# Second feed-forward weights by seven products per 2x2 block, and PSUM as one pool of banks

## The chip, the core and the metric

The kernel runs on one core of a Trainium2 chip. The core has a matrix engine (TensorE, PE in the profile, with its weight loads apart as PEld), VectorE (DVE), ScalarE (ACT), GpSimd (POOL) and SyncE (SP), which here only issues DMAs. Matrix products accumulate in PSUM, eight banks of 128 partitions by 512 fp32 numbers; everything else lives in SBUF. The metric is the device time of one execution in microseconds, the median of the runs.

## The reference, cut to what matters

Two blocks of two layers each work on x of 512 tokens by 1024 columns. Every layer has a mixer (convolution or attention) and then a feed-forward part; the first block also attends to a memory. The change is in the second products of the feed-forward parts (`@ w2`, `@ w_down`); their inner dimension is 4096 (`D_FF`) in the first block and 2816 (`D_FF_2`) in the second.

```python
def sqrelu_mlp(h, w1, w2):
    return jnp.square(jax.nn.relu(h @ w1)) @ w2

def swiglu(h, w_gate, w_up, w_down):
    return (jax.nn.silu(h @ w_gate) * (h @ w_up)) @ w_down

def first_block(...):
    for l in range(DEPTH):
        x = x + (conformer_conv(...) if l < N_A_LAYERS else fox_attention(...))
        x = x + memory_cross_attention(rmsnorm(x, norm_mem_g[l]), ...)
        x = x + sqrelu_mlp(rmsnorm(x, norm_ff_g[l]), ff_w1[l], ff_w2[l])
    return rmsnorm(x, final_norm_g)

def second_block(x, ...):
    for i in range(DEPTH):
        h = rms_norm(x, mix_norm[i])
        x = x + (short_conv_mixer(h, ...) if i % 2 == 0 else dilated_attention_mixer(h, ...))
        x = x + swiglu(rms_norm(x, ffn_norm[i]), ffn_w_gate[i], ffn_w_up[i], ffn_w_down[i])
    return rms_norm(x, final_norm)
```

## The kernel before

x stays in SBUF, transposed, as eight tiles `x0` to `x7` of 128 columns of the model by 512 tokens. Every fp32 operand of a large product is split in two numbers that the matrix engine takes at full rate, hi (the rounded value, a cast on ScalarE) and lo (the rest, a subtraction on VectorE): weights in `split_weights` (L163; `whi`, `wlo`, cast L169, subtraction L170), activations in `split_act` and `split_into` (L222 to L224; `ahi`, `alo`). `mm3` (L173) then makes one product of three matmuls, hi by hi, hi by lo, lo by hi, so that 24 matmuls of 512 columns make a block of 128 output columns from 1024 inputs.

`gemm_steps` goes over pairs of such output blocks. For a pair it loads 1 MB of weights from HBM (`load_weights`, tile `raw`, three buffers, issued by SP), splits it into four hi/lo tiles (two slots with two buffers each) and runs the products. `ff_sqrelu` works through the hidden dimension in four chunks of 1024: for each, the first weights give eight hidden tiles (evacuation L706, Square on ScalarE L708, split L224), and the second weights add the chunk's share to x (evacuation `residual`, L593: x = PSUM + x). `swiglu` does the same with gate and up weights, in chunks of 8, 8 and 6 hidden tiles. The norm's factor is computed while the first products run: at step 13 of the first gemm of a layer PE sums squares, POOL raises to the power -1/2 (`rtm`, L278), and at step 18 PE spreads the result over the partitions; every evacuation needs it.

PE runs its matmuls in the order in which the program writes them. The other engines' orders are made by a scheduler ahead of time from its own estimates; within an engine instructions start in that order, and a waiting instruction holds up all behind it. PSUM is opened anew by `banks(g, s, t)` where a stage starts: then the first matmul of the stage waits until the last bank of the stage before has been read.

The fox attention (`heads_attention`) starts with the splits of x without gain; the gains of its norm are multiplied into the weights instead (`gained`, L782, POOL; `fr`, L1119, POOL, for the forget gate's weights, which L1123 on VectorE finishes as tile `fw`).

## Time and profile before

| what | value |
|---|---|
| median of the three runs | 2654.21 us (2652.49 to 2655.27) |
| the profiled execution, its time | 2655.16 us |
| its span in the trace | 2653.4 us |
| granted TensorE clock, mean | 0.997 |
| PE busy | 2600.3 us, 98% |
| PEld busy | 2178.7 us, 82% |
| DVE busy | 1489.7 us, 56% |
| ACT busy | 1097.9 us, 41% |
| POOL busy | 548.8 us, 21% |

The span is the part of the execution that the trace covers; 1.76 us lie around it. Matmuls are pipelined, and each row of a matmul is drawn longer than the distance to the next one, so the distance between starts is what a matmul costs.

### The profile page before, as it was taken

To read this page: it belongs to the slowest core of one execution; us is meant where nothing else is said; L and a number is where in the kernel's file an instruction comes from. 1 tells how busy PE (TensorE), PEld (TensorE's weight loads), DVE (VectorE), ACT (ScalarE), POOL (GpSimd) and SP (SyncE) were. 2 spreads that over 40 slices of the span, in tenths; PEclk is the share of its full clock that TensorE was granted. 3 is DMA by queue.
4 is the path that set the end of the run, shared out by engine and by line. 5 is a ranking of instruction groups with operands and counts; after the bars stand their busy time and mean duration, and the time that the engine had idled before them with its cause. 6 is when DMAs were issued, how large, how long until landed. Compare 5 with 4: busy or idle time off the path is not lost.

```text
span 2653.4 us, 32283 instructions
## 1 busy us (share of the span) xinstructions
PE 2600.3 (98%) x12521; PEld 2178.7 (82%) x12521; DVE 1489.7 (56%) x2215; ACT 1097.9 (41%) x1843; POOL 548.8 (21%) x585
## 2 busy tenths in 40 slices
PE   8999999999999999999999999999999999999999
PEld 6889888888878787888888788888888888788888
DVE  6995564433557887554344665433335777643333
ACT  6755443322437675342223322322224666422223
POOL 5862110000226532110000511211112221211111
PEclk9999999999999999999999999999999999999999
DMA  7255133333322222233333393333324232233331
GB/s 211 78 194 181 56 96 96 98 103 101 95 74 72 80 96 72 72 111 96 95 97 96 87 166 109 90 100 101 96 83 119 85 88 88 77 96 98 96 87 56
DMA packets 319320, 264.82 MB, mean 100 GB/s; under 512 B 6980, under 2 KB 304512, under 8 KB 319168
## 3 DMA queue, kind: packets, MB, share of 16 engines
q1 hardware_dynamic: 316112, 258.15, 33.4%
q10 hardware_dynamic: 2480, 4.33, 0.5%
q8 instruction: 99, 1.62, 0.3%
q0 software_dynamic: 576, 0.28, 0.1%
q14 instruction: 53, 0.43, 0.1%
HBM read 251.16 MB, written 11.57 MB: 99 GB/s over the span
## 4 chain that ended last, share of the span: by engine, by line
PE 82%; DVE 6%; POOL 4%; issue 4%; ACT 2%; DMA 1%; SPq 0%; ACTq 0%; POOLq 0%; DVEq 0%
PE ps_g L92 76%; PE ps_s L92 3%; POOL pa L433 2%; PE ps_t L92 2%; PE ps_t L95 1%; DVE wlo L170 1%; DVE ps_s L425 1%; DVE alo L236 1%; DVE x L593 1%; POOL sall L994 1%; POOL raw L782 0%; DVE x L938 0%; DMA raw<-in_conv_pw_w 0%; DVE wlo L795 0%; DVE x L1286 0%
## 5 line engine op out<-in xcount | busy, mean ns | idle before, releaser
L92 PE MATMUL ps_g<-ahi,whi 128*128 128x512 f32 x3052 | 1195.2, 392 | 10.8 <-DVE x L593 5.8
L92 PE MATMUL ps_g<-alo,whi 128*128 128x512 f32 x3052 | 1188.0, 389 | 1.6 <-DVE alo L236 1.6
L92 PE MATMUL ps_g<-ahi,wlo 128*128 128x512 f32 x3052 | 1188.0, 389 | 0.0
L169 ACT CAST whi<-raw 128x1024 fp32r<-128x1024 f32 (+2 forms) x384 | 384.1, 1007 | 1163.1 <-PE ps_g L92 1103.3
L92 PEld LDWEIGHTS ps_g<-ahi,whi 128*128 128x128 f32 x3052 | 574.7, 188 | 129.6 <-issue 11.1
L92 PEld LDWEIGHTS ps_g<-ahi,wlo 128*128 128x128 f32 x3052 | 574.2, 188 | 120.3 <-DVE wlo L795 0.2
L92 PEld LDWEIGHTS ps_g<-alo,whi 128*128 128x128 f32 x3052 | 574.8, 188 | 117.5 <-DVE alo L236 2.4
L170 DVE TENSOR_TENSOR wlo<-raw,whi 128x1024 fp32r<-128x1024 f32 (+2 forms) x384 | 462.7, 1210 | 75.5 <-ACT whi L169 70.8
L593 DVE TENSOR_TENSOR x<-ps_g,x 128x512 f32<-128x512 f32 x144 | 99.1, 689 | 337.5 <-PE ps_g L92 337.5
L260 POOL TENSOR_TENSOR ssq<-ssq,sq 128x512 f32<-128x512 f32 x78 | 119.4, 1531 | 609.2 <-issue 311.9
L740 POOL TENSOR_TENSOR g<-g,rb 128x512 f32<-128x512 f32 x44 | 74.2, 1687 | 555.2 <-ACT g L739 555.2
L706 DVE SCALAR_TENSOR_TENSOR t<-ps_g,rb 128x512 f32<-128x512 f32 x64 | 44.0, 691 | 161.0 <-PE ps_g L92 160.3
L782 POOL TENSOR_TENSOR raw<-raw,gcols 128x512 f32<-128x512 f32 x48 | 53.8, 1145 | 302.1 <-DMA raw<-in_kvf_w 302.1
L433 POOL TENSOR_TENSOR pa<-pa,pr 128x512 f32<-128x512 f32 x80 | 111.8, 1400 | 18.7 <-ACT pa L429 8.2
L744 DVE TENSOR_TENSOR u<-ps_g,g 128x512 f32<-128x512 f32 x44 | 30.4, 691 | 145.3 <-PE ps_g L92 141.1
L425 DVE SCALAR_TENSOR_TENSOR ps_s<-u,gcols,ps_s 128x512 f32<-128x512 f32 x152 | 104.2, 744 | 0.2
L994 POOL TENSOR_SCALAR sall<-sall,rs 128x512 f32<-128x512 f32 (+3 forms) x128 | 75.9, 605 | 128.5 <-DVE rs L993 117.4
L795 DVE TENSOR_TENSOR wlo<-raw,whi 128x512 fp32r<-128x512 f32 x128 | 94.4, 765 | 13.2 <-ACT whi L792 13.2
L792 ACT CAST whi<-raw 128x512 fp32r<-128x512 f32 x128 | 74.1, 620 | 53.3 <-PE ps_g L92 47.1
L737 DVE TENSOR_TENSOR t<-ps_g,rb 128x512 f32<-128x512 f32 x44 | 30.4, 691 | 112.8 <-PE ps_g L92 112.8
L236 DVE SCALAR_TENSOR_TENSOR alo<-x,gcols,ahi 128x512 fp32r<-128x512 f32 x64 | 82.3, 1299 | 13.8 <-ACT ahi L235 13.8
L224 DVE TENSOR_TENSOR alo<-u,ahi 128x512 fp32r<-128x512 f32 x116 | 81.7, 707 | 2.7 <-ACT ahi L223 2.7
(244 smaller groups left out, 2838.0 us busy)
## 6 DMA issues: line engine op xcount, KB each, us to landing
raw<-in_ff_w SPq DMA_DIRECT2D x64, 1024.0 KB, 5.0
raw<-in_ffn_w_gate SPq DMA_DIRECT2D x44, 512.0 KB, 4.0
raw<-in_ffn_w_up SPq DMA_DIRECT2D x44, 512.0 KB, 5.3
raw<-in_ffn_w_down SPq DMA_DIRECT2D x16, 1024.0 KB, 5.0
raw<-in_conv_pw_w SPq DMA_DIRECT2D x16, 512.0 KB, 5.4
raw<-in_mem_wk SPq DMA_DIRECT2D x8, 1024.0 KB, 5.1
raw<-in_mem_wv SPq DMA_DIRECT2D x8, 1024.0 KB, 5.9
raw<-in_mem_wq SPq DMA_DIRECT2D x8, 1024.0 KB, 4.9
```

The costliest lines, as they stand in the source:

```text
L92: tc.keep_in_program_order(nc.tensor.matmul(*args, **kw))
L169: nc.scalar.copy(hi, view)
L170: nc.vector.tensor_tensor(lo, view, hi.bitcast(F32), op=OP.subtract)
L224: nc.vector.tensor_tensor(lo, src, hi.bitcast(F32), op=OP.subtract)
L236: nc.vector.scalar_tensor_tensor(lo, src, g, hi.bitcast(F32), op0=OP.mult, op1=OP.subtract)
L260: nc.gpsimd.tensor_tensor(self.ssq, self.ssq, dst, op=OP.add)
L425: nc.vector.scalar_tensor_tensor(acc, u[:, j : j + T], tapw(j), acc, op0=OP.mult, op1=OP.add)
L433: nc.gpsimd.tensor_tensor(pa, pa, pr, op=OP.add)
L593: nc.vector.tensor_tensor(x[m], acc, x[m], op=OP.add)
L740: nc.gpsimd.tensor_tensor(g, g, nrm.b, op=OP.mult)
L795: nc.vector.tensor_tensor(w[1][:, k0 : k0 + n, :], v, w[0][:, k0 : k0 + n, :].bitcast(F32), op=OP.subtract)
L994: pinned(nc.gpsimd.tensor_scalar(s, s, rs[:, i : i + 1], 1.0, op0=OP.mult, op1=OP.mult))
```

## The change

For all chunks of the feed-forward layers but each layer's last one, the second weights are multiplied by seven products per block of 2 by 2 instead of eight (Winograd's form of Strassen's scheme): input blocks in pairs, output blocks in pairs, tokens in halves of 256. `Hidden.quarters` makes the four differences of the activations' quarters; `Seven.weights` makes the four of the weights (one on POOL, three on VectorE) and splits seven weight blocks where four were split; `Seven.add` runs 7 products of 256 columns by four input pairs by three matmuls for each of the four output pairs j0 to j3. Two of the seven results go to x at once (`B`, `D` in `Seven.evac`), two are kept in accumulators `acc0` to `acc3` (`A`, `C`; copied by ScalarE in a layer's first chunk, added by VectorE later), and `Seven.combine` adds these to x; it is written into the last chunk's first gemm. In the first output pair, five products go over the first three input pairs before any of them takes the fourth. That is ten chunks: three in each `ff_sqrelu`, two in each `swiglu`; six of them are not their layer's first.

PSUM becomes one pool of eight banks with their own names, so that a bank waits only for its own last reader; `banks` deals them out by last use, and the bank that gathers values in `heads_attention` is kept out of the ring meanwhile (`held`). `gemm_steps` takes a bank when its first product comes. The feed-forward layers use six banks in the ring `g`, and the stage of the short convolution keeps these. The multiplications by the gain for the fox attention's first key and query weights and for `fr` move from POOL to VectorE.

```diff
@@ -106,18 +106,24 @@
...
-    psum = {}
+    psum = ExitStack()
+    ps_pool = pool("ps", stack=psum, space=bass.MemoryType.PSUM)
+    by_use = list(range(8))
+    rings, held = {}, set()
...
     def banks(g, s, t):
...
-        if psum:
-            psum["stack"].close()
-        psum["stack"] = ExitStack()
-        psum["pool"] = pool("ps", stack=psum["stack"], space=bass.MemoryType.PSUM)
-        psum["bufs"] = {"g": g, "s": s, "t": t}
+        free = list(by_use)
+        for tag, n in (("g", g), ("s", s), ("t", t)):
+            rings[tag], free = free[:n], free[n:]
...
     def bank(tag="g"):
-        return psum["pool"].tile([P, 512], F32, name="ps_" + tag, tag=tag, bufs=psum["bufs"][tag])
+        i = next(i for i in rings[tag] if i not in held)
+        rings[tag].remove(i)
+        rings[tag].append(i)
+        by_use.remove(i)
+        by_use.append(i)
+        return ps_pool.tile([P, 512], F32, name="ps_" + tag, tag=f"bank{i}", bufs=1)
...
@@ -188,10 +194,12 @@
...
-            acc = [bank("g") for _ in range(nm)]
+            acc = {}
...
             for k, m in order:
+                if m not in acc:
+                    acc[m] = bank("g")
                 mm3(acc[m], (w[m][0][:, k, :], w[m][1][:, k, :]), acts[k], k == 0, k == nk - 1)
...
@@ -595,6 +603,124 @@
...
+    SEVEN = (
+        ("b", None, 0, "A", 1),
+        ("a", 0, 2, "B", 1),
+        ("a", 1, 6, "D", 1),
+        ("c", 1, 4, "C", 1),
+        ("c", 0, 3, "C", 0),
+        ("d", 1, 5, "A", 0),
+        ("d", 0, 1, "B", 0),
+    )
+    HALF = T // 2
...
+    class Hidden:
...
+        def quarters(self):
+            f = self.raw
+            d = self.ap.tile([P, 4, HALF], F32, name="bdif", tag="bdif", bufs=1)
+            nc.scalar.copy(self.hi[:, 0:3, :], f[:, 1:4, :])
+            nc.vector.tensor_tensor(
+                d[:, 0:2, :], f[:, 1:3, :], f[:, 0:1, :].to_broadcast([P, 2, HALF]), op=OP.subtract
+            )
+            nc.vector.tensor_tensor(d[:, 2, :], f[:, 2, :], d[:, 0, :], op=OP.add)
+            nc.vector.tensor_tensor(d[:, 3, :], d[:, 2, :], f[:, 3, :], op=OP.subtract)
+            nc.scalar.copy(self.hi[:, 3:7, :], d)
+            for part, src in ((slice(0, 3), f[:, 1:4, :]), (slice(3, 7), d)):
+                nc.vector.tensor_tensor(
+                    self.lo[:, part, :], src, self.hi[:, part, :].bitcast(F32), op=OP.subtract
+                )
+
+    class Seven:
...
+            self.acc = [pl.tile([P, 4, HALF], F32, name=f"acc{j}", tag=f"acc{j}") for j in range(KT // 2)]
+            self.begun = False
...
+        def weights(self, src, r0, j, h):
+            raw = load_weights([(src, r0, 2 * j * P), (src, r0, (2 * j + 1) * P)], 2 * h)
+            v = raw[:, 0 : 2 * h, :].rearrange("p (i a) n -> p i a n", a=2)
+            even, odd = v[:, :, 0, :], v[:, :, 1, :]
+            a11, a21, a12, a22 = even[:, :, 0:P], even[:, :, P:], odd[:, :, 0:P], odd[:, :, P:]
+            w = {"b": split_weights(a11, [P, h, P]), "a": split_weights(odd, [P, h, 2 * P])}
+            nc.gpsimd.tensor_tensor(a21, a11, a21, op=OP.subtract)
+            nc.vector.tensor_tensor(a22, a22, a21, op=OP.subtract)
+            nc.vector.tensor_tensor(a11, a22, a11, op=OP.add)
+            nc.vector.tensor_tensor(a12, a12, a22, op=OP.subtract)
+            w["c"] = split_weights(even, [P, h, 2 * P])
+            w["d"] = split_weights(odd, [P, h, 2 * P])
+            return w
+
+        def add(self, src, r0, hid):
+            h = len(hid)
+            for j in range(KT // 2):
+                w = self.weights(src, r0, j, h)
+                ps = {}
+                order = [(i, k) for i in range(7) for k in range(h)]
+                if j == 0:
+
+                    order.sort(key=lambda ik: 2 if ik[0] > 4 else ik[1] == h - 1)
+                for i, k in order:
+                    grp, at, b, name, half = SEVEN[i]
+                    opens = name not in ps
+                    if opens:
+                        ps[name] = bank("g")
+                    wk = [z[:, k, :] if at is None else z[:, k, at * P : (at + 1) * P] for z in w[grp]]
+                    act = (hid[k].hi[:, b, :], hid[k].lo[:, b, :])
+
+                    closes = k == h - 1 and (name, half) in (("A", 0), ("B", 0), ("C", 0), ("D", 1))
+                    mm3(ps[name][:, half * HALF : (half + 1) * HALF], wk, act, opens, closes)
+                    if closes:
+                        self.evac(j, name, ps[name])
+            self.begun = True
...
+        def evac(self, j, name, b):
+            xe, xo, acc = x[2 * j], x[2 * j + 1], self.acc[j]
+            if name == "D":
+                nc.vector.tensor_tensor(xo[:, HALF:], xo[:, HALF:], b[:, HALF:], op=OP.subtract)
+            elif name == "B":
+                nc.vector.tensor_tensor(xe, b, xe, op=OP.add)
+            else:
+                a = flat(acc[:, 0:2, :] if name == "A" else acc[:, 2:4, :])
+                if self.begun:
+                    nc.vector.tensor_tensor(a, b, a, op=OP.add)
+                else:
+                    nc.scalar.copy(a, b)
+
+        def combine(self, j):
+            xe, xo, acc = x[2 * j], x[2 * j + 1], self.acc[j]
+            nc.vector.tensor_tensor(acc[:, 0, :], acc[:, 0, :], acc[:, 1, :], op=OP.add)
+            nc.vector.tensor_tensor(acc[:, 3, :], acc[:, 0, :], acc[:, 3, :], op=OP.add)
+            nc.vector.tensor_tensor(xe, xe, flat(acc[:, 0:2, :]), op=OP.add)
+            nc.vector.tensor_tensor(xe[:, 0:HALF], xe[:, 0:HALF], acc[:, 2, :], op=OP.subtract)
+            xv = xo.rearrange("p (a b) -> p a b", a=2)
+            nc.vector.tensor_tensor(xv, xv, acc[:, 3:4, :].to_broadcast([P, 2, HALF]), op=OP.add)
+            nc.vector.tensor_tensor(xo[:, 0:HALF], xo[:, 0:HALF], acc[:, 2, :], op=OP.subtract)
...
@@ -694,63 +820,81 @@
...
+            banks(6, 0, 2)
...
+            seven = Seven(fp)
             for hc in range(FF1 // D):
...
-                def evac(m, acc, hid=hid):
...
+                hid, parts = [], []
+                final = hc == FF1 // D - 1
...
+                def evac(m, acc, hid=hid, parts=parts, final=final):
+                    if m % 2 == 0:
+                        hid.append(Hidden(ap))
+                    t = hid[-1].place(m % 2)
                     nc.vector.scalar_tensor_tensor(t, acc, 0.0, nrm.b, op0=OP.max, op1=OP.mult)
-                    u = fp.tile([P, T], F32, name="u", tag="u", bufs=4)
-                    nc.scalar.activation(u, t, AF.Square)
...
-                gemm(cols(a["ff_w1"][l], 0, hc * D), h, evac, first=hc == 0, norm=nrm, hooks=nrm.hooks() if hc == 0 else ())
-                final = hc == FF1 // D - 1
-                gemm(
...
+                    nc.scalar.activation(t, t, AF.Square)
+                    if final:
+                        parts.append(hid[-1].tile(m % 2))
+                    elif m % 2:
+                        hid[-1].quarters()
+
+                hooks = nrm.hooks() if hc == 0 else ()
+                if final:
+                    hooks = [(8 + 12 * j, lambda j=j: seven.combine(j)) for j in range(KT // 2)]
+                gemm(cols(a["ff_w1"][l], 0, hc * D), h, evac, first=hc == 0, norm=nrm, hooks=hooks)
+                if final:
+                    gemm(cols(a["ff_w2"][l], hc * D, 0), parts, last or residual(st2), first=True)
+                else:
+                    seven.add(a["ff_w2"][l], hc * D, hid)
...
     def swiglu(l, st, last=None, finish=None):
...
-        banks(4, 2, 2)
+        banks(6, 0, 2)
...
                         if m == 0:
-                            t = fp.tile([P, T], F32, name="t", tag="t", bufs=4)
-                            nc.vector.tensor_tensor(t, acc, nrm.b, op=OP.mult)
-                            g = fp.tile([P, T], F32, name="g", tag="g", bufs=4)
-                            nc.scalar.activation(g, t, AF.Silu)
+                            nc.vector.tensor_tensor(g, acc, nrm.b, op=OP.mult)
+                            nc.scalar.activation(g, g, AF.Silu)
                             nc.gpsimd.tensor_tensor(g, g, nrm.b, op=OP.mult)
...
-                            nc.vector.tensor_tensor(u, acc, res[0], op=OP.mult)
-                            hid.append(split_act(ap, u))
+                            nc.vector.tensor_tensor(g, acc, g, op=OP.mult)
+                            if final:
+                                parts.append(hd.tile(e))
+                            elif e:
+                                hd.quarters()
...
+                    hooks = nrm.hooks() if first else ()
+                    if final and j < KT // 2:
+                        hooks = [(4, lambda j=j: seven.combine(j))]
+                    gemm([(wg, 0, c), (wu, 0, c)], h, evac, first=first, norm=nrm, hooks=hooks)
...
+                else:
+                    seven.add(wd, m0 * P, hid)
...
@@ -779,9 +923,11 @@
...
             def gained(v, k0, n):
-                ins = nc.gpsimd.tensor_tensor(
-                    v, v, f[:, k0 : k0 + n].unsqueeze(2).to_broadcast([P, n, width]), op=OP.mult
-                )
+                by = f[:, k0 : k0 + n].unsqueeze(2).to_broadcast([P, n, width])
+                if owner[:2] == ("kq", 1):
+                    nc.vector.tensor_tensor(v, v, by, op=OP.mult)
+                    return
+                ins = nc.gpsimd.tensor_tensor(v, v, by, op=OP.mult)
                 if owner[1] > 0:
                     pinned(ins)
...
@@ -881,6 +1027,8 @@
...
                     b = bank("g")
+                    own = by_use[-1]
+                    held.add(own)
...
                             if t2 == 1 and k == KT - 1:
                                 evac(tt, b)
+                                held.discard(own)
...
@@ -1116,7 +1265,7 @@
...
-            nc.gpsimd.tensor_tensor(fr, fr, gk.unsqueeze(2).to_broadcast([P, KT, 16]), op=OP.mult)
+            nc.vector.tensor_tensor(fr, fr, gk.unsqueeze(2).to_broadcast([P, KT, 16]), op=OP.mult)
...
@@ -1306,7 +1455,6 @@
...
-        banks(4, 2, 2)
```

What moves on VectorE, at three places (rows of the program's order; names carry buffer numbers where rows read alike otherwise).

The first place is VectorE in the third chunk of the first `ff_sqrelu`, in its second weights. Before, it adds finished PSUM banks to x and splits the next weights:

```order
L593 TENSOR_TENSOR x0_78<-ps_g_4945,x0_78 128x512
L593 TENSOR_TENSOR x1_79<-ps_g_4946,x1_79 128x512
L170 TENSOR_TENSOR wlo_5062<-raw_5059,whi_5061 128x1024
L170 TENSOR_TENSOR wlo_5066<-raw_5059,whi_5065 128x1024
L593 TENSOR_TENSOR x2_80<-ps_g_5007,x2_80 128x512
L170 TENSOR_TENSOR wlo_5124<-raw_5121,whi_5123 128x1024
```

Now, in the second pair j1 (`raw_5453`; L672 to L674 are the weights' differences, L176 the split, L707 the evacuation `B`, L717 to L723 the six instructions of `combine`):

```order
L707 TENSOR_TENSOR x0_78<-ps_g_5371,x0_78 128x512
L673 TENSOR_TENSOR raw_5453<-raw_5453 128x4x128
L674 TENSOR_TENSOR raw_5453<-raw_5453 128x4x128
L718 TENSOR_TENSOR acc0_3507<-acc0_3507 128x256
L719 TENSOR_TENSOR x0_78<-x0_78,acc0_3507 128x512
L176 TENSOR_TENSOR wlo_5570<-raw_5567,whi_5569 128x512
L722 TENSOR_TENSOR x1_79<-x1_79,acc0_3507 128x512
L176 TENSOR_TENSOR wlo_5468<-raw_5453,whi_5467 128x1024
L720 TENSOR_TENSOR x0_78<-x0_78,acc0_3507 128x256
```

The six instructions of `combine(0)`, which the program writes into the next chunk, stand here between those of the pair, and four of them lie ahead of `wlo_5468`, the lo part of the weights for the pair's fourth and fifth product.

The second place is VectorE in the same layer where the third chunk goes from the first weights to the second. Before, the last hidden tile is evacuated (L706) and split (L224):

```order
L706 SCALAR_TENSOR_TENSOR t_4927<-ps_g_4870,rb_3603 128x512
L170 TENSOR_TENSOR wlo_5004<-raw_4997,whi_5003 128x1024
L224 TENSOR_TENSOR alo_4932<-u_4929,ahi_4931 128x512
L593 TENSOR_TENSOR x0_78<-ps_g_4945,x0_78 128x512
L593 TENSOR_TENSOR x1_79<-ps_g_4946,x1_79 128x512
```

Now (L837 the evacuation, L647 to L651 the differences, L654 the lo parts of three and of four quarters, 768 and 1024 wide):

```order
L837 SCALAR_TENSOR_TENSOR braw_5301<-ps_g_5304,rb_3602 128x512
L176 TENSOR_TENSOR wlo_5358<-raw_5339,whi_5357 128x1024
L647 TENSOR_TENSOR bdif_5331<-braw_5301 128x512
L654 TENSOR_TENSOR blo_5300<-braw_5301,bhi_5299 128x768
L650 TENSOR_TENSOR bdif_5331<-braw_5301,bdif_5331 128x256
L651 TENSOR_TENSOR bdif_5331<-bdif_5331,braw_5301 128x256
L654 TENSOR_TENSOR blo_5300<-bdif_5331,bhi_5299 128x1024
```

Between the last evacuation and the last lo part of the activations there now stand a weight split, three instructions of differences and a split of 768.

The third place is VectorE ahead of the fox attention, where the last first-layer evacuations (L593, now L601) meet the splits for the next stage. Before:

```order
L593 TENSOR_TENSOR x_81<-ps_g,x_81 128x512
L170 TENSOR_TENSOR wlo<-raw,whi 128x1024
L224 TENSOR_TENSOR alo<-x_81,ahi 128x512
L593 TENSOR_TENSOR x_82<-ps_g,x_82 128x512
L795 TENSOR_TENSOR wlo<-raw,whi 128x512 x2
```

Now:

```order
L601 TENSOR_TENSOR x_81<-ps_g,x_81 128x512
L176 TENSOR_TENSOR wlo<-raw,whi 128x1024
L232 TENSOR_TENSOR alo<-x_81,ahi 128x512
L928 TENSOR_TENSOR raw<-raw,gcols 128x4x128 x2
L601 TENSOR_TENSOR x_82<-ps_g,x_82 128x512
L941 TENSOR_TENSOR wlo<-raw,whi 128x512 x2
L928 TENSOR_TENSOR raw<-raw,gcols 128x4x128 x2
L232 TENSOR_TENSOR alo<-x_82,ahi 128x512
```

The four multiplications by the gain (L928, before on POOL) stand among the evacuations of x, each pair ahead of the splits that need it.

## Rows read from the trace of the kernel before

**Rows 1.** Page, part 1: busy us, share of the span, instructions.

```profile
PE 2600.3 (98%) x12521; PEld 2178.7 (82%) x12521; DVE 1489.7 (56%) x2215; ACT 1097.9 (41%) x1843; POOL 548.8 (21%) x585
```

**Rows 2.** Waits of PE: line, releaser, us in total, times, the longest.

```profile
PE ps_g L92 <- DVE x L593: 5.8, 7, 1.5
...
PE ps_g L92 <- DVE x L1284: 5.1, 1, 5.1
...
PE ps_s L92 <- DVE fw L1123: 3.8, 1, 3.8
```

**Rows 3.** Timeline of PE in `ff_sqrelu`: start, duration, instruction; 512 columns.

```profile
1200.15 0.39 PE L92 MATMUL ps_g<-ahi,whi 128*128 128x512 f32 x1
...
1205.82 0.39 PE L92 MATMUL ps_g<-alo,whi 128*128 128x512 f32 x1
```

**Rows 4.** Timeline of PE in `heads_attention`, the same with 256 columns.

```profile
769.07 0.28 PE L92 MATMUL ps_g<-wlo,ahi 128*128 128x256 f32 x1
...
774.95 0.28 PE L92 MATMUL ps_g<-whi,alo 128*128 128x256 f32 x1
```

**Rows 5.** Windows: one second-weight stretch of `ff_sqrelu`; first row names the columns.

```profile
core 0: us, PE busy (x) PEld busy (x) DVE busy (x) ACT busy (x) POOL busy (x), PEclk, DMA share, GB/s
436.50:480.00 43.50, 43.50 (x194) 36.03 (x193) 15.93 (x18) 9.49 (x10) 0.00 (x0) 1.00 0.32 97
```

**Rows 6.** Groups of DVE instructions by shape: count, busy us, mean ns.

```profile
L593 DVE TENSOR_TENSOR x<-ps_g,x 128x512 f32<-128x512 f32 x144 | 99.1, 689 | 337.5 <-PE ps_g L92 337.5
...
L170 DVE TENSOR_TENSOR wlo<-raw,whi 128x512 fp32r<-128x512 f32 x32 | 21.8, 681 | 0.0
...
L224 DVE TENSOR_TENSOR plo<-ps_t,phi 128x256 fp32r<-128x256 f32 x32 | 13.2, 412 | 0.0
```

**Rows 7.** Tile `raw`, 395 to 470 us: min/median/max ns; landing in us.

```profile
L170 DVE TENSOR_TENSOR wlo<-raw,whi x15: 1207/1224/1226, 394.1 to 467.4; 128x1024 fp32r<-128x1024 f32 x15
...
L169 ACT CAST whi<-raw x14: 1039/1055/1056, 395.5 to 466.3; 128x1024 fp32r<-128x1024 f32 x14
...
DMA to landing us min/median/max: 4.8/4.9/6.6
```

**Rows 8.** Timeline of POOL at 740 us, start and duration.

```profile
740.14 1.45 POOL L260 TENSOR_TENSOR ssq<-ssq,sq 128x512 f32<-128x512 f32 x1 [3.99 <-ACT sq L256]
```

**Rows 9.** Timeline of DVE there, start and duration.

```profile
740.53 1.60 DVE L224 TENSOR_TENSOR alo<-x,ahi 128x512 fp32r<-128x512 f32 x1
...
745.13 9.68 DVE L795 TENSOR_TENSOR wlo<-raw,whi 128x512 fp32r<-128x512 f32 x2
```

**Rows 10.** Timeline of PE at the start of fox attention.

```profile
744.82 0.47 PE L92 MATMUL ps_g<-ahi,whi 128*128 128x512 f32 x1 [0.88 <-DVE x L593]
...
755.67 0.69 PE L92 MATMUL ps_s<-ahi,fw 128*64 128x512 f32 x1 [3.78 <-DVE fw L1123]
...
761.62 0.39 PE L92 MATMUL ps_s<-ahi,fw 128*64 128x512 f32 x1
```

**Rows 11.** Timeline of POOL there.

```profile
744.21 8.03 POOL L782 TENSOR_TENSOR raw<-raw,gcols 128x512 f32<-128x512 f32 x8
```

**Rows 12.** Windows: the matmuls after that wait; columns as in rows 5.

```profile
756.00:761.50 5.50, 5.50 (x14) 2.91 (x13) 0.00 (x0) 0.00 (x0) 0.00 (x0) 0.50 0.73 189
```

**Rows 13.** Timeline of PE at the start of the short convolution.

```profile
1492.33 0.77 PE L92 MATMUL ps_g<-ahi,whi 128*128 128x512 f32 x1 [5.05 <-DVE x L1284]
...
1495.42 0.39 PE L92 MATMUL ps_g<-alo,whi 128*128 128x512 f32 x1
```

**Rows 14.** Timeline of POOL there.

```profile
1495.53 1.30 POOL L260 TENSOR_TENSOR ssq<-ssq,sq 128x512 f32<-128x512 f32 x1 [1.09 <-ACT sq L256]
```

**Rows 15.** Timeline of PE inside fox attention, a wait and what followed.

```profile
892.68 1.20 PE L95 MATMUL ps_t<-mats,sall 128*128 128x128 f32 x9 [2.42 <-POOL sall L994]
```

**Rows 16.** Timeline of POOL at the first `ff_sqrelu`: the norm's factor.

```profile
403.86 1.02 POOL L278 TENSOR_TENSOR rtm<-ms,mhalf 128x4 f32<-128x4 f32 x1 [4.52 <-DVE ms L276]
```

**Rows 17.** Timeline of PE there: the matmuls that spread it.

```profile
406.94 0.83 PE L92 MATMUL ps_t<-mats,rtm 128*128 128x128 f32 x6
```

**Rows 18.** Timeline of SP there: the load of the first second-weight pair.

```profile
398.22 0.37 SPq L150 DMA_DIRECT2D raw<-in_ff_w  x1
```

More of the change, by code (lines that the diff above doesn't have):

```diff
@@ L597, in residual, with flat, __init__, place @@
         return evac
+    SEVEN = (
[8 more added lines that the diff above has]
+    HALF = T // 2
+    def flat(v):
+        return v.rearrange("p a b -> p (a b)")
+    class Hidden:
+        def __init__(self, ap):
+            self.ap = ap
+            self.hi = ap.tile([P, 7, HALF], F32R, name="bhi", tag="bhi", bufs=4)
+            self.lo = ap.tile([P, 7, HALF], F32R, name="blo", tag="blo", bufs=4)
+            self.raw = ap.tile([P, 4, HALF], F32, name="braw", tag="braw", bufs=3)
+        def place(self, e):
+            return flat(self.raw[:, 2 * e : 2 * e + 2, :])
+        def tile(self, e):
+            hi, lo = (flat(z[:, 2 * e : 2 * e + 2, :]) for z in (self.hi, self.lo))
+            split_into(hi, lo, self.place(e))
+            return hi, lo
+        def quarters(self):
[12 more added lines that the diff above has]
+                )
@@ L696, in ff_sqrelu @@
         with ExitStack() as s:
-            ap = pool("fact", 22, s)
+            banks(6, 0, 2)
+            ap = pool("fact", stack=s)
             fp = pool("fftmp", stack=s)
@@ L719, in swiglu @@
         nrm = Norm(st)
-        banks(4, 2, 2)
+        banks(6, 0, 2)
         with ExitStack() as s:
-            ap = pool("gact", 22, s)
+            ap = pool("gact", stack=s)
             fp = pool("gtmp", stack=s)
@@ L1404, in tokens @@
                 for j in range(2):
-                    b = bank("gs"[j])
+                    b = bank("g")
                     for k in range(4):
@@ L1425, in model_kernel @@
     swiglu(1, st, last2, finish)
-    psum["stack"].close()
+    psum.close()
     es.close()
```

29 lines of the change are left out of this document (13 added, 16 removed).

## The prediction

> **What bounds the kernel now.** I read the page first: PE is busy for 98% of the span, VectorE for 56% [rows 1]. Then the waits of PE: few are long, and three groups of them sit at starts of stages (x of L593, x of L1284, `fw` of L1123) [rows 2]. So the kernel goes at the pace of TensorE, and the stretch that is changed does so more than most: in one whole second-weight stretch PE is busy all 43.50 us, VectorE for 15.93 [rows 5]. What counts there is the distance of matmuls: 512 columns come every 5.67/25 = 0.2268 us (26 starts from first to last) [rows 3], 256 columns, each with a weight load of its own, every 5.88/49 = 0.120 us (50 starts) [rows 4]. Half the width thus costs 0.53 of the whole.
>
> **What the seven products save.** A second-weight chunk has 8 blocks of 24 matmuls: 192 x 0.2268 = 43.55 us, which the window agrees with [rows 5]. Now it has 4 pairs x 7 products x 4 input pairs x 3 = 336 matmuls of 256 columns: 336 x 0.120 = 40.32, or 10.08 a pair. That is 3.23 less in each of ten chunks: -32.3 us. The saving is small (7 x 0.53 against 4), so a few us of waiting in a chunk eat it.
>
> A rule of the Trainium skill speaks against the change: "TensorE: Matmul & The Clock Gate", section "Back-to-back issue gap", says that in a stream of loads and matmuls both set the distance, about 81 ns at 128 columns and 131 ns at 512. Put on a line (an estimate from that page) this is 98 ns at 256, so that 336 x 0.098 = 32.9 would stand against 192 x 0.131 = 25.2: a loss of 7.7 a chunk, and a sum of about 2755 instead of the one below. This trace does not agree with its figures (0.2268 at 512), and the 256-column row decides. I take -32.3.
>
> **What the start of a chunk costs.** Let F be the end of the last first-weight matmul; all times in this and the next part count from it. The last evacuation takes VectorE to 0.9 (a matmul's row is 0.16 longer than the distance [rows 3], so some 0.2, and 0.69, the price of 512 columns [rows 6]). Then, as the second piece of the order shows, a weight split of 1024 (1.22 [rows 7]) while ScalarE squares, differences of 512, 256 and 256, and a split of 768 (0.95, between 0.68 and 1.22): 0.69 + 0.41 + 0.41 + 0.95 more, to 4.6; ScalarE casts 1024 in 1.055 [rows 7] with handovers that I estimate at those 0.2 on either side, to 6.0; the lo part takes 1.22: 7.2. TensorE has 15 threefold products without the fourth input pair, 15 x 0.36 = 5.4, and comes to the first that needs this lo part at 6.2. Stall 1.0. In `swiglu` no Square stands ahead, I take 0.85. Six and four times: +9.4. At the lower end it is 0 (if VectorE gets ahead of the split of weights), at the upper 1.6 each.
>
> **What the pairs cost VectorE.** A pair takes TensorE 10.08 us. VectorE has for it four weight splits (0.68 + 3 x 1.22 [rows 6, 7]), three differences (3 x 0.69) and evacuations of 256 and three times 512 (0.41 + 3 x 0.69): 8.9. That fits alone. But the order (first piece) puts `combine` of each pair into the same layer's last seven-product chunk, not after it: its six instructions are 4 x 0.41 + 2 x 0.69 = 3.0 [rows 6], and that is 11.9 against 10.08. The order has it so in four chunks, the third of each `ff_sqrelu` and the second of each `swiglu`.
>
> There VectorE is busy without a pause from 7.2 on. Up to the lo part for pair j1's fourth product stand 10.6 us of work, so it is there at 17.8; TensorE needs it at 1.0 + 10.08 + 12 x 0.36 + 0.12 = 15.5: stall 2.3. Up to the same part for pair j3 I count three splits of 512, nine of 1024, 13 instructions of 256 and 24 of 512 columns: 3 x 0.68 + 9 x 1.22 + 13 x 0.41 + 24 x 0.69 = 34.9, so 42.1; TensorE without stalls in the pairs would need it at 1.0 + 30.24 + 4.32 + 0.12 = 35.7. In all 6.4 late: 2.3 in j1 and 4.1 in j3. After j3 the next chunk's evacuations leave room, and nothing further is late.
>
> To this comes POOL. Its one difference per pair runs beside VectorE: a subtraction of 0.68 took 1.60 while POOL worked on a tensor of 512 columns [rows 8, 9]. The load for j3 is issued when j0's last weights are split (2.1) and lands 4.9 later [rows 7], so one such meeting falls into the stretch: 0 to 0.9, I take 0.5. Thus +6.9 in each of four chunks, +27.6. In the two plain chunks of `ff_sqrelu` that add to accumulators, the same walk ends level at j1 (15.55 against 15.5); with half of POOL's price +0.5 each, +1.0. In the four first chunks ScalarE copies, and there is room.
>
> **What the pool of banks and the moves give.** At the fox attention PE waits 0.88 for the last x and 3.78 for `fw`; then 14 steps take 5.95 where they would take 3.18 [rows 10]: the granted clock is 0.50 there [rows 12], the 1.2 GHz level, after the idle time. VectorE sat in L795 for 9.68 [rows 9] behind POOL's eight multiplications, 8.03 long, that begin only at 744.21 [rows 11]. With the multiplications on VectorE among its evacuations (third piece of the order), `fw` is ready at about 749, before TensorE comes to it near 751: -0.88 - 3.78 - 2.77 = -7.4. At the short convolution the wait of 5.05 for the last bank goes and with it seven steps at the lower clock, 3.09 for 1.59 [rows 13]; but the column sums then come at about 1495.4 and need the sum that POOL ends at 1496.83 [rows 14], a new wait of 1.4: -5.05 - 1.5 + 1.4 = -5.15. Of the other 4.9 us behind L593 [rows 2] I take a quarter, -1.2; the rest waits for data, not for banks. Together -13.8, between -5 (if what is late next takes it over) and -17.
>
> POOL's first difference stands ahead of the norm's factor in its queue: the load issued at 398.22 [rows 18] lands 4.9 to 6.6 later [rows 7], the difference ends at 404.1 to 406.3 with POOL's 1.0 to 1.45 [rows 8, 11], the factor 1.02 later [rows 16], and TensorE needs it at 406.94 [rows 17]. With the slowest load 0.4 shows, in two layers. I take 0.
>
> **Sum.** 2655.16 (profiled) - 32.3 + 9.4 + 27.6 + 1.0 - 13.8 = 2647.1. The median of the runs lies 0.95 below the profiled one, so 2646.
>
> **Rivals.** (1) The clock falls in j3. The 4.1 us there come as about 0.5 (ScalarE's cast), one matmul, and 3.6. After 2.42 of idle time matmuls went on at the full rate [rows 15], after 3.78 and 5.05 they did not [rows 10, 13]; 3.6 lies close to the upper. Each such fall costs up to 2.8 as at `fw`: four times 11, to 2658, within my measure of no change or just slower. This is the main danger, and it decides if the stall passes about 3.7. (2) The combining costs nothing: VectorE's small instructions go faster or the stalls merge with those at the start; then 28 fall away: 2619. For it speaks that the 6.4 is a difference of two large sums, 5% of 34.9 are 1.7; against it that a sum of 12 per pair cannot fit in 10.08. (3) Slower: VectorE is the bound in every pair. This is decided where a plain pair costs it more than 10.08, now 8.9; if every instruction beside POOL or ScalarE were longer by 20% (in the quiet stretch the 1024 split keeps within 1.21 to 1.23 [rows 7], which gives no sign of it), 24 begun pairs would lose 0.6 and the combined chunks 7 more: +42, 2688. (4) The stage starts keep their waits: +9 to +14, 2658. (5) TensorE is held by loads: their mean is 2178.7/12521 = 0.174 [rows 1]; if they did not overlap, a chunk would be 58.5 instead of 40.3 and the whole 2829. Milder, half-wide matmuls at more than 43.55/336 = 0.130 would end the saving, and at 0.154 (8 more a chunk) the time would be 2758. The 256-column row at 0.120 speaks against both, and I give them 0.01 together. (The rule of the Trainium skill above is of the milder kind.) Not making its change is no case: the matmuls are counted.
>
> **Chances.** My forecast 0.42 (its own range 2640 to 2654); clock 0.18; no cost of combining, or smaller stalls, 0.20; VectorE the bound 0.10; stage starts 0.08; loads 0.01, others 0.01. A difference of 0.2%, 5.3 us, is about what a measurement here can tell from none. Faster than 2648.9: most of the forecast's (0.27) and the 0.20, 0.47; within: 0.14 and 0.12 from clock and starts, 0.26; slower: 0.27. Leaving out VectorE's far end and half of the cheapest case gives 2615 to 2672.
>
> **What would show it.** Right: 256-column starts 0.12 apart; each chunk begins with a wait of about 1 us on `blo`; in the four chunks PE waits for `wlo`, L176, some 2 us in j1 and 4 in j3; no wait on `fw`. Wrong: a PEclk under 1 in j3 (rival 1), no waits on `wlo` (2), waits for `wlo` in other pairs (3).

## The result, and the profile after

Before 2654.7 us (median of the 4 runs beside it, 2652.5 to 2656.4), after 2634.7 us (4 runs, 2633.0 to 2635.6). The ratio is 0.9928, 95% interval 0.9913 to 0.9943: 20 us faster. The profiled execution of after took 2632.98 us, its span 2631.2. One of the twelve executions of experiment 4 below took 5510.6 us, twice as long as any other, and is left out of its median.

Part 1 of the page of after answers to [rows 1]:

```profile
PE 2571.9 (98%) x13961; PEld 2224.3 (85%) x13961; DVE 1785.1 (68%) x2684; ACT 1205.6 (46%) x1955; POOL 601.8 (23%) x620
```

PE has 1440 matmuls more, since the seven products' are half as wide, and is busy for 28.4 us less; VectorE has 295 us more to do and is still far from full on the average.

The waits of PE in after (line, releaser, us in total, times, the longest), which answer to [rows 2]:

```profile
PE ps_g L92 <- DVE wlo L176: 12.3, 8, 1.8
...
PE ps_g L92 <- DVE alo L244: 5.4, 4, 2.2
PE ps_g L92 <- DVE blo L654: 4.8, 10, 0.6
...
PE ps_s L92 <- DVE fw L1272: 1.4, 1, 1.4
```

The waits on x (L593 and L1284 of before) are gone, `fw` is down from 3.8 to 1.4. New are ten waits on `blo`, one at each chunk's start, and eight on the weights' lo part, L176: two in each of the four combined chunks.

Windows of after (columns as in rows 5): from the first chunk's start to its end, then the third chunk, with `combine` in it.

```profile
441.40:475.00 33.60, 33.60 (x280) 33.60 (x281) 25.94 (x31) 17.93 (x22) 1.30 (x1) 1.00 0.34 106
610.00:645.00 35.00, 31.78 (x260) 31.27 (x260) 34.45 (x54) 12.32 (x14) 1.31 (x1) 1.00 0.21 65
```

In the first, 33.60/280 = 0.120 us a matmul: the half-wide distance of [rows 4] holds where each matmul brings a new weight. In the second VectorE is busy for 34.45 of 35 us: here it is the bound, while its mean over the span is 68%.

The timeline of PE shows what the waits cost (start, duration, and in brackets the idle time before). First a chunk's start, then waits in combined chunks: both of the first such chunk, with the matmul behind the second, and the longest, with the matmul ahead of it:

```profile
440.49 0.28 PE L92 MATMUL ps_g<-bhi,whi 128*128 128x256 f32 x1
441.32 0.39 PE L92 MATMUL ps_g<-blo,whi 128*128 128x256 f32 x1 [0.55 <-DVE blo L654]
...
620.40 0.39 PE L92 MATMUL ps_g<-bhi,wlo 128*128 128x256 f32 x1 [1.09 <-DVE wlo L176]
...
642.40 0.39 PE L92 MATMUL ps_g<-bhi,wlo 128*128 128x256 f32 x1 [1.58 <-DVE wlo L176]
642.62 0.28 PE L92 MATMUL ps_g<-bhi,whi 128*128 128x256 f32 x1
...
1883.80 0.28 PE L92 MATMUL ps_g<-blo,whi 128*128 128x256 f32 x1
1885.85 0.39 PE L92 MATMUL ps_g<-bhi,wlo 128*128 128x256 f32 x1 [1.76 <-DVE wlo L176]
```

What a wait costs is the distance to the matmul before it less the usual 0.120: 441.32 - 440.49 - 0.12 = 0.71 at the first start, 1885.85 - 1883.80 - 0.12 = 1.93 at the longest. That is some 0.16 more than the bracket, whose idle time begins only when the row of the matmul before ends. All waits together, by this measure: at the starts 0.71 in six chunks and 0.52 to 0.53 in four, 6.4; in the combined chunks 1.25, 1.66, 1.93 and 1.75 in j1 and 1.73 or 1.74 four times in j3, 13.5.

### The profile page after: what moved, and what is told of

It is laid out like the page before. It is cut to its first block, busy times and chain, and to the rows that moved or that the text cites. A ratio compares the mean times of both kernels' runs of the same rounds, so it can differ in the third digit from the quotient of the medians.

```text
span 2631.2 us, 35659 instructions
## 1 busy us (share of the span) xinstructions
PE 2571.9 (98%) x13961; PEld 2224.3 (85%) x13961; DVE 1785.1 (68%) x2684; ACT 1205.6 (46%) x1955; POOL 601.8 (23%) x620
## 3 DMA queue, kind: packets, MB, share of 16 engines
q1 hardware_dynamic: 316112, 258.15, 33.6%
## 4 chain that ended last, share of the span: by engine, by line
PE 79%; DVE 11%; issue 4%; POOL 3%; ACT 3%; DMA 1%; SPq 0%; POOLq 0%; DVEq 0%; ACTq 0%
PE ps_g L92 72%; PE ps_s L92 3%; DVE wlo L176 2%; DVE ps_s L433 2%; PE ps_t L92 2%; PE ps_t L95 2%; POOL pa L441 1%; DVE blo L654 1%; ACT whi L175 1%; POOL sall L1143 1%; DVE alo L244 0%; ACT bhi L652 0%; DVE x L1435 0%; DMA raw<-in_conv_pw_w 0%; DVE x L601 0%
## 5 line engine op out<-in xcount | busy, mean ns | idle before, releaser
L92 PE MATMUL ps_g<-ahi,whi 128*128 128x512 f32 x2176 | 856.3, 394 | 0.0
L92 PE MATMUL ps_g<-alo,whi 128*128 128x512 f32 x2176 | 850.6, 391 | 5.4 <-DVE alo L244 5.4
L92 PE MATMUL ps_g<-ahi,wlo 128*128 128x512 f32 x2176 | 850.1, 391 | 0.2 <-DVE wlo L941 0.2
L176 DVE TENSOR_TENSOR wlo<-raw,whi 128x1024 fp32r<-128x1024 f32 (+2 forms) x464 | 549.7, 1193 | 81.1 <-ACT whi L175 77.6
L92 PEld LDWEIGHTS ps_g<-ahi,whi 128*128 128x128 f32 x2176 | 410.0, 188 | 82.5 <-ACT whi L938 0.2
L92 PE MATMUL ps_g<-bhi,wlo 128*128 128x256 f32 (+1 forms) x1356 | 407.7, 301 | 12.3 <-DVE wlo L176 12.3
L92 PE MATMUL ps_g<-blo,whi 128*128 128x256 f32 (+1 forms) x1356 | 407.8, 301 | 4.8 <-DVE blo L654 4.8
L92 PE MATMUL ps_g<-bhi,whi 128*128 128x256 f32 (+1 forms) x1356 | 406.9, 300 | 0.0
L92 PEld LDWEIGHTS ps_g<-bhi,wlo 128*128 128x128 f32 x1356 | 259.9, 192 | 22.1 <-DVE wlo L176 13.9
L92 PEld LDWEIGHTS ps_g<-blo,whi 128*128 128x128 f32 x1356 | 260.0, 192 | 15.5 <-DVE blo L654 6.8
L92 PEld LDWEIGHTS ps_g<-bhi,whi 128*128 128x128 f32 x1356 | 260.0, 192 | 8.7
L837 DVE SCALAR_TENSOR_TENSOR braw<-ps_g,rb 128x512 f32<-128x512 f32 x64 | 44.0, 691 | 118.9 <-PE ps_g L92 118.2
```

Of the source, the lines that this page charges most:

```text
L92: tc.keep_in_program_order(nc.tensor.matmul(*args, **kw))
L176: nc.vector.tensor_tensor(lo, view, hi.bitcast(F32), op=OP.subtract)
L837: nc.vector.scalar_tensor_tensor(t, acc, 0.0, nrm.b, op0=OP.max, op1=OP.mult)
```

## Why: the theory and its rivals

The theory to be tested had three parts. **A:** in the four combined chunks VectorE sets the time, and all of the 13.5 is due to `combine` being there. **B:** the chunk starts wait for the last lo part on VectorE, 6.4. **C:** the pool of banks and the moves give some 13.8 by themselves, as predicted, so that the seven products gain only the small rest. The rivals: the waits on L176 come from late loads or from weights freed late, and would stay without `combine`; or the seven products give most of the 20 us, the banks little.

## Experiments

Times are medians of several runs; the kernel before stood at 2654.8 beside experiments 1 to 4 and at 2654.6 beside 5 to 8, and each ratio is to those.

**1. `combine` kept out of the last chunk's seven products.** Its six additions, and the evacuations of the last chunk's first-weight products behind which they stand in the program, keep their program order, so that they run after the stretch, under the last chunk's wide matmuls. The diff shows one of the six and one of the two evacuations.

```diff
-            nc.vector.tensor_tensor(acc[:, 0, :], acc[:, 0, :], acc[:, 1, :], op=OP.add)
+            pinned(nc.vector.tensor_tensor(acc[:, 0, :], acc[:, 0, :], acc[:, 1, :], op=OP.add))
...
-                    nc.vector.scalar_tensor_tensor(t, acc, 0.0, nrm.b, op0=OP.max, op1=OP.mult)
+                    ins = nc.vector.scalar_tensor_tensor(t, acc, 0.0, nrm.b, op0=OP.max, op1=OP.mult)
+                    if final:
+                        pinned(ins)
```

> The six instructions of each combine and the last chunk's evacuations are held in the program's order on VectorE, so that none of them stands among the seven products any more. If VectorE is late there because of them, the eight waits on wlo (12.3 us) and the half-clock stretch behind one of them (1.55) go: 2634.7 - 13.9 = about 2621. Rival: the waits are due to the seven products' own splits and differences, or the combining makes the last chunk's evacuations late instead: 2630 to 2636.

Measured 2620.35 (2618.0 to 2621.0), ratio 0.9870 [0.9858, 0.9883], 14.3 us under after. The waits of PE in this kernel have no row for L176 any more; the starts' row is as it was:

```profile
PE ps_g L92 <- DVE blo L654: 4.8, 10, 0.6
```

A holds: 13.5 of waiting and 1.5 of lower clock behind the longest of them (below) are 15.0, of which 14.3 came back. In this kernel the first layer's `combine` runs from 650 to 681 us, under the last chunk's wide matmuls. Loads and the rings of weights were not touched, so they were not what was late.

**2. All seven products' last input pair put off in a chunk's first pair,** not only that of five, so that the lo part is asked for later.

```diff
-                    order.sort(key=lambda ik: 2 if ik[0] > 4 else ik[1] == h - 1)
+                    order.sort(key=lambda ik: ik[1] == h - 1)
```

> In a chunk's first pair all seven products, not five, go over the first three input pairs before any takes the fourth; nothing else is changed. If the wait at a chunk's start is the lo part of the last activations coming late, the six further threefold products (2.2 us) hide it and the ten waits on blo (0.52 to 0.71 each, 6.3 in all) go: about 2628.5. Rival: the sixth and seventh product's weights are then late instead, and the time stays at 2634 to 2636.

Measured 2662.26, ratio 1.0025 [1.0014, 1.0035]: a miss by 34 us, and slower than before. Its waits of PE:

```profile
PE ps_g L92 <- DVE wlo L176: 17.9, 16, 2.5
PE ps_g L92 <- ACT whi L175: 13.6, 10, 2.2
```

The waits on `blo` are gone, as meant, but 26 waits for weights stand in their place: 31.5 us where after has 17.1 on `blo` and weights together. That is half of the loss, for the profiled execution is 30.5 us longer than that of after. The other half goes with the granted clock, 0.989 on the mean where after has 0.997; by the distances of matmul starts the 1.2 GHz level costs this kernel some 14 us more than after. Experiments 6 to 8 go on from here.

**3. The eight wide products of before with the pool of banks and the moves.** `ff_sqrelu` and `swiglu` are those of before, with the six banks of after; all else is as after.

```diff
-            ap = pool("fact", stack=s)
+            ap = pool("fact", 22, s)
...
-                    seven.add(a["ff_w2"][l], hc * D, hid)
+                gemm(
+                    cols(a["ff_w2"][l], hc * D, 0), hid, (last or residual(st2)) if final else residual(None), first=True
+                )
```

> The pool of banks, the ring of six and the moves from POOL to VectorE stay; the feed-forward layers compute with eight products as before. By the traces the seven products save 32.3 and lose 6.3 at chunk starts, 13.5 on wlo and 1.55 to the clock, net -10.9, so the rest gives about -9: about 2645.5. By the prediction's terms the seven products lose 5.7 and the rest gives all: 2634 to 2641.

Measured 2641.31 (2640.8 to 2643.4), ratio 0.9953 [0.9941, 0.9964]: -13.5 us. C holds. It is the number that the prediction's terms gave for the banks and the moves, not that of the traces' sum (2645.5): the seven products gain less than the -10.9 of that sum, 6.6 us in place.

**4. The seven products alone,** PSUM closed and opened anew for each stage as before (six banks for the products in these two), the fox multiplications on POOL.

```diff
-        i = next(i for i in rings[tag] if i not in held)
-        rings[tag].remove(i)
...
+        return psum["pool"].tile([P, 512], F32, name="ps_" + tag, tag=tag, bufs=psum["bufs"][tag])
...
-                if owner[:2] == ("kq", 1):
-                    nc.vector.tensor_tensor(v, v, by, op=OP.mult)
-                    return
```

> The seven products with PSUM opened anew per stage as before (six banks in the feed-forward layers) and the multiplications by the gain back on POOL. If the parts add up, this has the seven products' -10.9: about 2644. Rival: the two parts need each other (a stage start that waits for VectorE's longer queue): 2650 or more.

Measured 2649.70, ratio 0.9981 [0.9972, 0.9990]: -5.1 us, next to the rival's 2650. Its waits of PE:

```profile
PE ps_g L92 <- DVE wlo L170: 12.6, 8, 2.0
...
PE ps_g L92 <- DVE x L595: 6.0, 4, 2.3
...
PE ps_s L92 <- DVE fw L1260: 4.9, 1, 4.9
PE ps_g L92 <- DVE blo L648: 4.7, 10, 0.6
PE ps_g L92 <- DVE x L1421: 4.4, 1, 4.4
```

The waits inside the seven products are those of after (12.6 and 4.7 for 12.3 and 4.8), and the three at stage starts of [rows 2] are back. The two parts hardly act on each other: -13.5 - 5.1 = -18.6, together they gave -20.1. So the rival's number came without the rival's reason: what was wrong is the -10.9. Part of what it left out is the granted clock, 0.993 on the mean where before has 0.997; by the distances of matmul starts the 1.2 GHz level costs some 7 us more here than in before. Two thirds of the gain come from the banks and the moves; the seven products, which are most of the diff, bring 5 to 7 us.

**5. Only the fox moves undone:** the gains of its key and query columns and of its gate columns are multiplied on POOL again.

```diff
-                if owner[:2] == ("kq", 1):
-                    nc.vector.tensor_tensor(v, v, by, op=OP.mult)
-                    return
...
-            nc.vector.tensor_tensor(fr, fr, gk.unsqueeze(2).to_broadcast([P, KT, 16]), op=OP.mult)
+            nc.gpsimd.tensor_tensor(fr, fr, gk.unsqueeze(2).to_broadcast([P, KT, 16]), op=OP.mult)
```

> The changed kernel with the gains of the fox stage's key and query columns and of its gate columns multiplied on GpSimd again; the pool of banks and the seven products stay. The prediction's term for the fox start was 7.4, of which the moves carry 5.9 (the wait on fw and the half clock behind it) and the banks the rest. By it 2640.6 (2639 to 2642), with a wait on fw of some 4 to 5 us in place of 1.4. Rival, the pool of banks alone had already freed that start (evacuations earlier, so the gains end in time): 2634.7.

Measured 2643.84 (2641.0 to 2646.0), ratio 0.9960 [0.9946, 0.9973]: 9.2 us over after, 3.3 more than expected, within what the two intervals leave open. One row of its waits, and a window behind that wait (columns as in rows 5):

```profile
PE ps_s L92 <- DVE fw L1269: 4.9, 1, 4.9
```

```profile
749.50:753.00 3.50, 3.50 (x10) 1.85 (x11) 0.00 (x0) 0.00 (x0) 0.00 (x0) 0.55 0.98 257
```

The wait is back (4.9 for 1.4) and with it the 1.2 GHz level behind it: the start of the fox stage is 5.0 longer in this profile than in that of after. The rest lies in stretches that the edit does not touch, where the granted clock fell at other places than in after; I can't assign it. The banks without the moves free the x wait, not the `fw` wait.

**6. Experiment 1 with VectorE's order at a chunk's start mended.** In `quarters()` the three differences and the two lo parts keep their program order; the diff shows one of the five.

```diff
-            nc.vector.tensor_tensor(d[:, 2, :], f[:, 2, :], d[:, 0, :], op=OP.add)
+            pinned(nc.vector.tensor_tensor(d[:, 2, :], f[:, 2, :], d[:, 0, :], op=OP.add))
```

> The kernel combine_late (2620.4) with the VectorE work on a chunk's last pair of hidden tiles kept in the order in which the code has it: the three differences first, then the two lo parts. Theory, the order on VectorE makes the chunk start late: the 128x768 lo part stood between the differences and held back bdif, and with it ScalarE's cast and the 128x1024 lo part that TensorE waits for, by 0.86 us from start to start, more than the excess of 0.71 (six chunks) and 0.52 (four). So the ten waits on blo go, 6.3 us: 2614. Rival 1, the chain from the bank to the lo part is bounded by ScalarE and the order is not what is late: 2620. Rival 2, the 128x768 part is then late itself: the waits come back on it, 2617 to 2620.

Measured 2615.34 (2611.4 to 2616.4), ratio 0.9851 [0.9837, 0.9864]: the fastest kernel of this study, 5.0 under experiment 1 and 39 under before. No row of its waits names `blo`, and of 12.3 us on L176 0.2 are left. The timeline of VectorE at the first chunk's start, in after:

```profile
437.18 0.95 DVE L654 TENSOR_TENSOR blo<-braw,bhi 128x768 fp32r<-128x768 f32 x1
438.05 0.42 DVE L650 TENSOR_TENSOR bdif<-braw,bdif 128x256 f32<-128x256 f32 x1
438.50 0.43 DVE L651 TENSOR_TENSOR bdif<-bdif,braw 128x256 f32<-128x256 f32 x1
440.04 1.23 DVE L654 TENSOR_TENSOR blo<-bdif,bhi 128x1024 fp32r<-128x1024 f32 x1 [1.11 <-ACT bhi L652]
```

and in this kernel:

```profile
437.78 0.42 DVE L650 TENSOR_TENSOR bdif<-braw,bdif 128x256 f32<-128x256 f32 x1
438.24 0.43 DVE L651 TENSOR_TENSOR bdif<-bdif,braw 128x256 f32<-128x256 f32 x1
438.58 0.95 DVE L654 TENSOR_TENSOR blo<-braw,bhi 128x768 fp32r<-128x768 f32 x1
439.78 1.23 DVE L654 TENSOR_TENSOR blo<-bdif,bhi 128x1024 fp32r<-128x1024 f32 x1 [0.25 <-ACT bhi L652]
```

In after VectorE does the 768 lo part first and then idles 1.11 for ScalarE's cast of the last difference; here it does the 768 lo part during that cast, and idles 0.25. B holds, and it was the order of two instructions.

**7. One late product early:** the sixth product's first input pairs stand ahead of the five's last one. **8. The same together with experiment 1.**

```diff
-                    order.sort(key=lambda ik: 2 if ik[0] > 4 else ik[1] == h - 1)
+                    order.sort(key=lambda ik: 0 if ik[0] < 5 and ik[1] < h - 1 else 1 if ik[0] == 5 and ik[1] < h - 1 else 2)
```

> The changed kernel, with one of the two late products (the sixth) given its first k's ahead of the five's last k in a chunk's first pair. That puts off the first use of the last lo part by 9 steps, 1.08 us, more than the excess of 0.71. Theory for seven_first3 (2662): its chunk starts were clean, but the first pair's a weights came free only 1.4 us before the pair's end instead of 3.6, and the second pair's split, 1.05 on ScalarE and 1.22 on VectorE, came late for them. Here they come free 2.5 us before the end: late enough in the second pair for no wait or a small one. So 2628.5 (6.3 less than 2634.7), at worst 2632. Rival, it is the third bank or the d weights, asked for earlier, that cost seven_first3 its time: then this kernel loses too, 2640 or more.

> combine_late and one_early together: combine is held out of the last chunk's seven products, and the sixth product's first k's stand ahead of the five's last k in a chunk's first pair. By the theory of one_early 6.3 less than 2620.4: 2614; if the second pair's weights are late by a little, up to 2618; if the third bank or the d weights are what cost seven_first3 its time, 2625 or more.

Measured 2645.07, ratio 0.9961 [0.9948, 0.9973], 10.4 over after; with experiment 1 2630.48, 0.9906 [0.9892, 0.9919], 10.1 over it. Both missed. Waits of PE with the edit alone, then with experiment 1:

```profile
PE ps_g L92 <- DVE wlo L176: 10.9, 8, 2.2
PE ps_g L92 <- ACT whi L175: 8.2, 6, 2.0
```

```profile
PE ps_g L92 <- DVE wlo L176: 7.2, 12, 1.0
...
PE ps_g L92 <- ACT whi L175: 2.0, 6, 0.7
```

So it is again the weights, even without `combine`, but with the edit alone their waits are the smaller part of the loss: on `blo` and weights together they are 19.1 us where after has 17.1, and the profiled execution is 8.6 longer. The larger part is TensorE's clock. In each of the four combined chunks two waits of about 2.0 and 2.1 stand close together (in the third chunk at 622.19 and 624.80), and behind them matmuls run at the 1.2 GHz level. Windows of 12 us around the waits in j1 of the third chunk, in after and in experiment 7:

```profile
618.00:630.00 12.00, 10.90 (x91) 10.70 (x91) 12.00 (x20) 4.19 (x5) 0.00 (x0) 1.00 0.27 87
620.00:632.00 12.00, 7.93 (x45) 7.52 (x45) 9.57 (x14) 3.99 (x4) 0.00 (x0) 0.72 0.28 87
```

In the other three combined chunks the clock of such a window is 0.86, 0.72 and 0.72, in after 1.00, 0.86 and 1.00. With experiment 1 the clock does not fall inside the chunks: there the waits grow from 4.8 to 9.2, the ten chunks are 6.0 longer by their matmuls' starts, and the rest of its loss lies elsewhere.

The timeline of VectorE in the third chunk says why one late release is more than one late split. In after:

```profile
611.91 0.69 DVE L711 TENSOR_TENSOR acc<-ps_g,acc 128x512 f32<-128x512 f32 x1 [0.30 <-PE ps_g L92]
612.51 1.22 DVE L176 TENSOR_TENSOR wlo<-raw,whi 128x1024 fp32r<-128x1024 f32 x1
```

in experiment 7:

```profile
614.18 1.28 DVE L711 TENSOR_TENSOR acc<-ps_g,acc 128x512 f32<-128x512 f32 x2
615.38 1.22 DVE L176 TENSOR_TENSOR wlo<-raw,whi 128x1024 fp32r<-128x1024 f32 x1
```

The last `blo` before these rows begins at 609.37 in after and at 611.34 in experiment 7. From it to the lo part of the next pair's `a` weights it is 3.14 in after and 4.04 in experiment 7. The `a` weights come free later, both accumulators' additions stand ahead of their lo part, and the three differences and two more splits of that pair follow only then. My expectation priced one split and left out the chain behind it and the clock. Experiment 6 takes the same wait at the start away without letting the weights go later, and gained 5.0 of the 6.3 expected: that speaks for the release as the cause. What each of the three, release, queue order and clock, costs was not separated by an experiment; a third buffer for the `a` weights would do it, and was not tried.

## Why the prediction was right, and where its terms were off

**The time fell as forecast, by more than the sum had it.** 2646 was predicted, 2634.7 measured: inside the whole range of 2615 to 2672, but 5 us below the forecast's own 2640 to 2654, on the side of rival 2 (no cost of combining, or smaller stalls; 0.20). The mechanisms were the ones named; a term was mis-sized.

**The products, -32.3: right.** The 256-column distance was to be 0.120, and is. By the Trainium skill ("TensorE: Matmul & The Clock Gate", section "Back-to-back issue gap") an estimate of 98 ns stood against 131 ns for the wide ones, a loss; the trace of after does not agree any more than that of before did (120 ns and 227 ns).

**The combined chunks, +27.6: the place and the cause right, the size not; measured 13.5, and 1.5 of lower clock.** The step that failed is the walk of VectorE up to pair j3: "3 x 0.68 + 9 x 1.22 + 13 x 0.41 + 24 x 0.69 = 34.9". These are durations of rows. The timeline of VectorE in after, the walk's first and last row and a piece of it:

```profile
610.51 0.69 DVE L176 TENSOR_TENSOR wlo<-raw,whi 128x512 fp32r<-128x512 f32 x1
...
618.52 0.69 DVE L722 TENSOR_TENSOR x<-x,acc 128x512 f32<-128x512 f32 x1
619.12 1.22 DVE L176 TENSOR_TENSOR wlo<-raw,whi 128x1024 fp32r<-128x1024 f32 x1
620.26 0.42 DVE L720 TENSOR_TENSOR x<-x,acc 128x256 f32<-128x256 f32 x1
620.60 0.42 DVE L705 TENSOR_TENSOR x<-x,ps_g 128x256 f32<-128x256 f32 x1
...
641.12 1.23 DVE L176 TENSOR_TENSOR wlo<-raw,whi 128x1024 fp32r<-128x1024 f32 x1
```

Back to back, 512 columns take 0.60 from start to start, 1024 take 1.14 and 256 take 0.34, while the rows are drawn at 0.69, 1.22 and 0.42: each overlaps the next by about 0.085. Over 48 steps that is 4.1, of which short pauses, that the prediction took as none, give 1 back: the walk took 642.35 - 610.51 = 31.8 instead of 34.9. That is 3.1 of the 3.5 us a chunk by which the sum was too high. The rest is the meeting with POOL, priced at 0.5: POOL's one difference in the stretch (611.34, 1.31 us) met instructions that read a PSUM bank (L705, L711), and these kept their length. The trace of before had the overlap of rows too (its timeline of VectorE):

```profile
393.53 0.68 DVE L593 TENSOR_TENSOR x<-ps_g,x 128x512 f32<-128x512 f32 x1
394.13 1.21 DVE L170 TENSOR_TENSOR wlo<-raw,whi 128x1024 fp32r<-128x1024 f32 x1
395.27 0.68 DVE L593 TENSOR_TENSOR x<-ps_g,x 128x512 f32<-128x512 f32 x1
```

For TensorE the prediction took the distance of starts and not the rows; for VectorE it took the rows. Rival 2 had priced it so ("5% of 34.9 are 1.7"); the error was 9%.

**The chunk starts, +9.4: measured 6.4,** 0.71 and 0.53 for 1.0 and 0.85, and not by VectorE's rows but by the handovers. In after, the first narrow matmul of the first chunk and ScalarE's cast of the differences:

```profile
434.38 0.28 PE L92 MATMUL ps_g<-bhi,whi 128*128 128x256 f32 x1
```

```profile
438.96 1.05 ACT L652 CAST bhi<-bdif 128x1024 fp32r<-128x1024 f32 x1 [2.15 <-DVE bdif L651]
```

VectorE's last difference (438.50, 0.43 long, in experiment 6) ends 4.55 after that matmul begins, where 4.6 was forecast. From there to the cast, and from the cast's end to the lo part at 440.04, it is 0.03 each, where the prediction estimated 0.2 on either side. That is the 0.3; the chain of the `swiglu` chunks was not followed. The plain chunks, +1.0: nothing.

**Banks and moves, -13.8: experiment 3 gave -13.5.** That the sum agrees so well is partly luck, for its parts do not. At `fw` 1.4 of waiting is left where none was forecast; at the short convolution it is 0.5 for the column sums where 1.4 was forecast. New are waits where a norm's lo part is late after each attention, in after:

```profile
1007.78 0.50 PE L92 MATMUL ps_g<-alo,whi 128*128 128x512 f32 x1 [0.43 <-DVE alo L244]
1011.69 0.50 PE L92 MATMUL ps_g<-alo,whi 128*128 128x512 f32 x1 [2.24 <-DVE alo L244]
```

They took the place of waits on x of about the same sum, so the quarter that was booked there (1.2) did not come from there.

**Rival 1, a falling clock in j3: not there, but once in j1.** Windows of after, 3.1 us behind the wait of 1.93 and behind j3's of 1.74:

```profile
1885.90:1889.00 3.10, 3.10 (x17) 3.10 (x18) 3.10 (x5) 0.00 (x0) 0.00 (x0) 0.58 0.03 10
642.40:645.50 3.10, 3.10 (x26) 3.10 (x27) 3.10 (x5) 0.29 (x1) 0.00 (x0) 1.00 0.06 12
```

Only the first has the 1.2 GHz level for most of the window, 17 matmuls where 26 fit; until it ended it cost 1.5. The bounds that the prediction took, idle times of 2.42 without a fall and 3.78 with one, lay above the 1.76 of this wait: a shorter wait can cost the clock. Nor does its length alone settle it. In experiment 5 the same wait of the same chunk is longer, 1.94, and no fall follows:

```profile
1896.37 0.38 PE L92 MATMUL ps_g<-bhi,wlo 128*128 128x256 f32 x1 [1.94 <-DVE wlo L176]
```

```profile
1896.40:1899.50 3.10, 3.10 (x26) 3.10 (x27) 3.10 (x5) 0.00 (x0) 0.00 (x0) 1.00 0.05 15
```

So the 1.5 in after is in part chance: another kernel with this wait had none of it. **Rival 3, VectorE the bound in each pair: no**; the first chunk's window, without `combine`, has it busy for 25.9 of 33.6. **Rivals 4 and 5: no**, by experiment 3 and the distance.

**The sum with measured terms:** 2655.2 - 32.3 + 6.4 + 13.5 + 1.5 - 13.5 = 2630.8, against 2633.0 for the profiled execution. Of the 2.2 left over 1.8 are in the rows: behind each of the 18 waits the next matmul comes after 0.22 and not after 0.12 (642.40 and 642.62 above), and these 0.10 are not in the measure of a wait.

## What to carry to other kernels

Work out an engine's walk from the distance of starts of back-to-back rows, on every engine; row durations gave 34.9 us for VectorE's 49 instructions here, which took 31.8, and the error doubled a term that was the small difference of two long sums. When one algorithm trades TensorE time for work on VectorE, ask where in the program the extra work lands and not only how much it is: the same additions cost 14 us under narrow matmuls and nothing under wide ones. And before an operand's use is put off, see whose buffer it holds: one wait of 0.7 us was traded for late weights and, behind their longer waits, for TensorE's lower clock.
